# Splitting the sums of a slab's first pair of rows behind half of the down products, with five split weight pairs and four loaded tiles

## The chip, the cores and the metric

The kernel runs on one core of a Trainium2 chip. The metric is the device time of one execution in microseconds. The core has five engines with instruction queues of their own: TensorE (PE) for matmuls, with its weight loads shown as PEld, VectorE (DVE), ScalarE (ACT), GpSimd (POOL) and SyncE (SP), which here issues nearly all loads and stores. Each engine works through its queue in order, so an instruction that waits holds up all that stand behind it on its engine.

## The reference

One decoder layer for 1056 tokens (1024 of a prompt, eight sequences of four sampled tokens) of 1024 channels, in float32. Cut to what matters here:

```python
h = _rms(x, n_mix_pre); z = h @ w_in
m = concat([attention(q, k, v), pooling_mixer(u)]) @ w_out
x = x + _rms(m, n_mix_post)
f = _rms(x, n_ffn_pre)
f = (silu(f @ w_gate) * (f @ w_up)) @ w_down      # 1024 -> 2816 -> 1024
x = x + _rms(f, n_ffn_post)
x = x + sigmoid(x @ w_ple_gate) * (p @ w_ple)
```

It also returns the updated key, value and pooling windows.

## The kernel before, in words

**Numbers as pairs.** TensorE works on a rounded form of float32. To keep the precision, each operand is split into a rounded high part and the rest: `split(hi, lo, src)` (lines 163 to 165) is a copy on ACT (L164) and a subtraction on DVE (L165). A product then takes three matmuls: high by high, high by low, low by high. All of them come from line 126.

**Weights.** SP loads a weight tile of 512 KB into a `wr` tile; `W_RAW = 3` of these exist. A split turns it into a pair `wh`, `wl` of `wp` tiles; `2 * W_PAIRS = 8` of these exist. When a buffer is asked for again, the writer waits until the last reader of its former content is done. In the projections `weights(j, ahead=W_PAIRS - 1)` splits tiles ahead. In the channel sub-layer (FFN) the tiles are listed in `ITEMS`, and `need(k)` (lines 264 to 276) makes all items up to `LOOK = 4` beyond the one asked for.

**The FFN loop.** The tokens form three groups of 352; the first two share a scheme with seven instead of eight block products, the third is computed directly. The 22 blocks of 128 hidden channels form 11 slabs of two rows ("pairs" of a gate and an up weight; slot 0 and slot 1). `WALK` makes 16 visits: slabs 0 to 4 for the third group alone, slabs 5 to 10 for all three, then slabs 0 to 4 again for groups 0 and 1. Each row needs, for groups 0 and 1, sums of quarters of its gate and up weights: `w_sums` (lines 980 to 997) makes them by four POOL adds (L990) in place in the two loaded tiles, and splits both results (`sh` on ACT, `sl` on DVE). The adds can only start when the ordinary splits of the same tiles have read them.

A row is computed by `gate_up` (lines 1006 to 1069): products B11 and B21 of the gate weight, SiLU into `c`, for slot 0 then the *pending* down products of the visit before, then T4 with the up weight and S2, S3, S1, S4 with the sums. The adds of L1024 collect them from PSUM; the results are the hidden tiles `hid`, of group 0 (`hid<-c`) and of group 1 (`hid<-u`), split too. `downs(n)` (lines 1133 to 1143) runs over the output rows m = 0 to 3, then 4 to 7, and in each half over the groups 2, 0, 1; each product of six matmuls goes to one of eight PSUM banks, and DVE adds it to `o` (L1087), which frees the bank.

**Other work among it.** When the third group's last down products are done, the closing norm and the gate of that group (`ple_steps(2)`, with L1115 and L1119 on DVE) are issued a step at a time between the products; `turn` and `chain` count matmuls and DVE load for that. L1115 reads the broadcast norm factor from a PSUM bank.

**What sets the order.** The order of TensorE's matmuls is pinned to the written one. On the other engines, apart from a few pinned operations, a scheduler arranges the instructions when the program is built, from what they depend on and from its own estimates; their order can differ from the written one.

Of the kernel before, what the change touches and what calls it, by code (L numbers as in the profile page):

```python
# [47 lines left out]
UEXT = PST + DSEQ  # L48
ULEN = UPRE + SEQ + NDEC * UEXT

W_PAIRS = 4
W_RAW = 3


WARM = 8
# [6 lines left out]
def trunk_kernel(  # L62
# [31 lines left out]
    nc = tc.nc  # L94
# [11 lines left out]
    def nm(s):  # L106
        cnt[0] += 1
        return f"{s}{cnt[0]}"

    def act_tile(shape, dt=F32, s="a"):  # L110
        return apool.tile(shape, dt, tag="a", bufs=A_SLOTS, name=nm(s))
# [51 lines left out]
    def split(hi, lo, src):  # L163
        fix(se.copy(hi, src))  # L164
        fix(ve.tensor_tensor(lo, src, hi.bitcast(F32), op=ALU.subtract))  # L165
# [3 lines left out]
    def w_load(j):  # L169
        if j >= len(plan) or j in raws:  # L170
            return
        src, shape = plan[j]
        t = wpool.tile(shape, F32, tag="wr", bufs=W_RAW, name=nm("wr"))
        nc.sync.dma_start(t, src)
        raws[j] = t

    def w_tile(shape, s):
        return wpool.tile(shape, F32R, tag="wp", bufs=2 * W_PAIRS, name=nm(s))

    def w_split(j):  # L180
        if j >= len(plan) or j in pairs:
            return
        w_load(j)
        shape = plan[j][1]
        hi, lo = w_tile(shape, "wh"), w_tile(shape, "wl")
        split(hi, lo, raws[j])
        pairs[j] = (hi, lo)

    lazy = [False]

    def weights(j, ahead=W_PAIRS - 1):
        for i in range(j, j + (0 if lazy[0] else ahead) + 1):
            w_split(i)
            w_load(i + 1)
        return pairs[j]
# [19 lines left out]
    WALK += [(s, (0, 1)) for s in range(AHEAD)]  # L215
    ITEMS = []

    def item(kind, *js):
        ITEMS.append((kind, js))
        return len(ITEMS) - 1  # L220

    def direct_item(src, shape):
        return item("direct", add_plan(src, shape))

    WGU, WD = [], []
    for s, gs in WALK:
        pairs_of = []
        for i in range(SLAB):
            c = SLAB * s + i
            jg = direct_item(w_gu[c, 0], [P, KC, P])  # L230
            if 0 not in gs:
                ju = direct_item(w_gu[c, 1], [P, KC, P])
            if i == 0 and WD:
                last_s = WALK[len(WD) - 1][0]
                WD[-1] = [direct_item(w_dn[last_s, j], [P, SLAB, 512]) for j in range(2)]
            if 0 in gs:
                ju = direct_item(w_gu[c, 1], [P, KC, P])
            js = item("sums", jg, ju) if 0 in gs else None
            pairs_of.append((jg, ju, js))
        WGU.append(pairs_of)  # L240
        WD.append(None)
# [17 lines left out]
            wp = direct_item(w_ple[0], [P, 2, 512])  # L259
        WPE[1][m] = wp, direct_item(w_pg[m], [P, KC, P])  # L260

    made = {}

    def need(k, ahead=LOOK):

        for i in range(len(made), min(k + ahead + 1, len(ITEMS))):
            kind, js = ITEMS[i]
            if kind == "direct":
                w_split(js[0])
                made[i] = pairs[js[0]]  # L270
            else:
                made[i] = w_sums(*(raws[ITEMS[j][1][0]] for j in js))
            for kind, js in ITEMS[i + 1 : i + 3]:
                if kind == "direct":
                    w_load(js[0])
        return made[k]

    def gemm(ps, ops, start=True, stop=True):

        last = len(ops) - 1  # L280
        for i, (wh, wl, xh, xl) in enumerate(ops):
            mm(ps, wh, xh, start=start and i == 0, stop=False)
            mm(ps, wh, xl, start=False, stop=False)
            mm(ps, wl, xh, start=False, stop=stop and i == last)
# [56 lines left out]
    def load(dst, src):  # L341
        tc.keep_in_program_order(nc.sync.dma_start(dst, src))  # L342
# [38 lines left out]
    def u_load(c, h):  # L381
        j = U0[c]
        if h == 0:
            shape = plan[j][1]
            raws[j] = act_tile(shape) if c == 3 else wpool.tile(shape, F32, tag="wr", bufs=W_RAW, name=nm("wr"))
        load(raws[j][:, 4 * h : 4 * h + 4, :], plan[j][0][:, 4 * h : 4 * h + 4, :])
# [34 lines left out]
    for dst, src in ((psc, pscale), (skp, sink_p), (skd, sink_d)):  # L421
        load(dst, src)
    wpl = wpool.tile([P, 4, P], F32, tag="wr", bufs=W_RAW, name="wpl")
    nc.sync.dma_start(wpl, w_pool)
# [462 lines left out]
    def chain(steps, wait=0, alone=False):  # L887

        chains.append([steps, now[0] + wait, alone])
# [74 lines left out]
    for m in range(4, KC):  # L964
        out_proj(m, 1)
        need(0, m - 4)
        turn(24)
# [12 lines left out]
    def w_sums(a1, a2):  # L980


        a11, a12, a21, a22 = a1[:, 0:4, :], a1[:, 4:8, :], a2[:, 0:4, :], a2[:, 4:8, :]
        for out, a, b, op in (
            (a22, a21, a22, ALU.add),
            (a21, a11, a21, ALU.subtract),
            (a11, a22, a11, ALU.subtract),
            (a12, a12, a11, ALU.subtract),
        ):
            ge.tensor_tensor(out, a, b, op=op)  # L990
        two = []
        for src in (a1, a2):
            hl = w_tile([P, KC, P], "sh"), w_tile([P, KC, P], "sl")
            split(*hl, src)
            two.append(hl)
        (s24, s31) = two
        return {"S2": quarter(s24, 0), "S4": quarter(s24, 1), "S3": quarter(s31, 0), "S1": quarter(s31, 1)}

    def ops4(w, x):

# [2 lines left out]
    def quarter(w, h):  # L1003
        return tuple(t[:, 4 * h : 4 * h + 4, :] for t in w)

    def gate_up(items, slot, gs, pending):
# [16 lines left out]
        def add(out, a, ps):  # L1023
            ve.tensor_tensor(out, a, ps, op=ALU.add)  # L1024

        wg = need(ig)
        if 0 in gs:
            p1 = tmp(n, "p1")
# [8 lines left out]
        if pending and 0 in gs:  # L1037
            pending()
        wu = need(iu)
        if 2 in gs:  # L1040
            ve.tensor_tensor(sl, sl, direct(wu), op=ALU.mult)
# [59 lines left out]
    def ple_steps(g):  # L1101

        pl = half(g, F32R, "pl")
        pls[g] = pl[:, 0:2, :], pl[:, 2:4, :]
        raw = act_tile([P, 2, NS[g]])
        nc.sync.dma_start(raw, p[:, :, OFF[g] : OFF[g + 1]])
        x2s[g] = []
        for h in range(2):
            x2[g][h] = half(g, s="x2")
            nc.sync.dma_start(x2[g][h], x1d[g][h])  # L1110
        r = yield from rstd_steps(acc3[g])
        behind = tc.keep_in_program_order if g == 2 else lambda ins: ins
        for h in range(2):
            yh, xh = os_[g][h], x2[g][h]
            behind(ve.tensor_tensor(yh, yh, bc4(r), op=ALU.mult))  # L1115
            for c in range(4):
                k = 4 * h + c
                behind(
                    ve.scalar_tensor_tensor(  # L1119
                        xh[:, c, :], yh[:, c, :], gn[:, 3, k : k + 1], xh[:, c, :], op0=ALU.mult, op1=ALU.add  # L1120
                    )
                )
                if g == 2 and c % 2:
                    yield 6, 0
            yield 12 if g == 2 else 24, 0
            x2s[g].append(f_operand(xh, g))
            yield 10, 0
        split(*pls[g], raw)
        yield 6, 0
# [3 lines left out]
    def downs(n):  # L1133
        s, gs = WALK[n]
        hid[:] = old_hid
        for half_m in (range(4), range(4, KC)):
            for g in (2, 0, 1):
                for m in half_m:
                    if g in gs:
                        (last_down if g == 2 and s == NSLAB - 1 else down)(n, m, g)  # L1140
        if s == NSLAB - 1:
            share[0] = 0.1
            chain(ple_steps(2), 19)

    for n, (s, gs) in enumerate(WALK):
        if n == AHEAD:
            finish(list(chains))
        old_hid = list(new_hid)
        for i in range(SLAB):
            gate_up(WGU[n][i], i, gs, (lambda: downs(n - 1)) if i == 0 and n else None)  # L1150
# [126 lines left out]
```

## Time and profile before

| | before |
|---|---|
| median of 3 runs | 1118.11 us (1117.52 to 1119.99) |
| profiled execution | 1118.37 us |
| its span | 1116.6 us |
| mean granted TensorE clock | 0.998 |
| PE busy | 1106.5 us, 99% of the span |
| DVE busy | 748.3 us, 67% |
| ACT busy | 440.0 us, 39% |
| POOL busy | 179.4 us, 16% |
| read from and written to HBM | 88.30 MB and 10.11 MB |

The times in the profile count from the start of the span; 1.8 us of the execution lie around it. The channel sub-layer's first visits begin at about 220, the visits with groups 0 and 1 alone run from about 800 to 1000, and the last down products and the output part follow. In a row of the timeline stand the start, the duration, the engine, the line, the operation with its output and inputs, and in brackets the idle time of the engine before it with the instruction that ended it. In a row of waits stand who waited for whom, and then the sum, the number and the longest of these waits in us.

### The profile page before, as it was taken

Reading aid. Unit: us, or ns where it says so; the run is one execution under the profiler, and the core shown is the slowest. Engines: PE = TensorE matmul, PEld = TensorE weight load, DVE = VectorE, ACT = ScalarE, POOL = GpSimd, SP = SyncE. Lnnn points to the kernel's source line nnn. Section 1 sums busy time; section 2 is a strip of 40 time slices with the busy share of each in tenths; the row PEclk is TensorE's granted clock in tenths of the full one; section 3 lists DMA queues with packets and bytes.
Section 4 is the critical chain, followed back from the end, with each engine's and each line's share of the span. In section 5 each row is a group of like instructions: output and inputs, shape, how many; then the busy total and the mean of one; then the engine's idle time right before and its main releaser. Section 6 shows DMA issues by size and latency. Waiting matters only on the chain.

```text
span 1116.6 us, 17703 instructions
## 1 busy us (share of the span) xinstructions
PE 1106.5 (99%) x7171; PEld 1089.6 (98%) x7171; DVE 748.3 (67%) x1241; ACT 440.0 (39%) x779; POOL 179.4 (16%) x152
## 2 busy tenths in 40 slices
PE   8999999999999999999999999999999999999998
PEld 8999988899999999999999999999999999999998
DVE  6667478886979955255564555547887877789532
ACT  8323276664645523331222313123424334365220
POOL 0045032200000131011111102112132123100000
PEclk9999999999999999999999999999999999999999
DMA  8121311542543212121120202122112222336211
GB/s 289 56 71 38 122 43 38 194 157 85 203 166 129 99 38 76 39 76 39 38 60 17 78 36 76 38 100 79 57 58 83 70 76 80 124 133 222 85 58 39
DMA packets 35217, 99.54 MB, mean 89 GB/s; under 512 B 4132, under 2 KB 14660, under 8 KB 35136
## 3 DMA queue, kind: packets, MB, share of 16 engines
q1 hardware_dynamic: 33808, 96.65, 25.5%
q10 hardware_dynamic: 1328, 1.77, 0.5%
q8 instruction: 56, 0.92, 0.3%
q14 instruction: 25, 0.20, 0.1%
HBM read 88.30 MB, written 10.11 MB: 88 GB/s over the span
## 4 chain that ended last, share of the span: by engine, by line
PE 93%; DVE 3%; DMA 1%; issue 1%; POOL 1%; ACT 1%; SPq 0%; DVEq 0%; POOLq 0%
PE b L126 92%; PE b L120 1%; DMA xr<-in_x_dram 1%; DVE wl L165 1%; POOL wr L990 0%; SPq L342 0%; DVE h L368 0%; DVE o L1115 0%; DVE x L1119 0%; DVE mx L628 0%; DVE a L736 0%; DVE p L1024 0%; DVE hid L165 0%; ACT h L366 0%; ACT xr L377 0%
## 5 line engine op out<-in xcount | busy, mean ns | idle before, releaser
L126 PE MATMUL b<-fh,wh 128*128 128x352 f32 x808 | 260.7, 323 | 0.0
L126 PE MATMUL b<-fh,wl 128*128 128x352 f32 x808 | 259.3, 321 | 0.0
L126 PE MATMUL b<-fl,wh 128*128 128x352 f32 x808 | 259.0, 321 | 0.0
L126 PE MATMUL b<-hid,wh 128*128 128x352 f32 x1056 | 252.5, 322 | 1.8 <-DVE o L1115 1.2
L164 ACT CAST wh<-wr 128x1024 fp32r<-128x1024 f32 (+1 forms) x139 | 143.0, 1031 | 248.9 <-PE b L126 205.6
L165 DVE TENSOR_TENSOR wl<-wr,wh 128x1024 fp32r<-128x1024 f32 (+1 forms) x139 | 170.5, 1229 | 57.9 <-ACT wh L164 53.9
L126 PEld LDWEIGHTS b<-hid,wh 128*128 128x128 f32 x1056 | 182.3, 188 | 2.6 <-issue 1.5
L126 PE MATMUL b<-hid,wl 128*128 128x352 f32 x528 | 169.0, 320 | 0.0
L990 POOL TENSOR_TENSOR wr<-wr 128x512 f32<-128x512 f32 x44 | 63.4, 1441 | 623.0 <-DVE wl L165 621.3
L126 PEld LDWEIGHTS b<-fl,wh 128*128 128x128 f32 x808 | 151.9, 188 | 0.0
L126 PEld LDWEIGHTS b<-fh,wl 128*128 128x128 f32 x808 | 151.8, 188 | 0.0
L126 PEld LDWEIGHTS b<-fh,wh 128*128 128x128 f32 x808 | 151.6, 188 | 0.0
L1087 DVE TENSOR_TENSOR o<-o,b 128x352 f32<-128x352 f32 x240 | 114.9, 516 | 29.3 <-PE b L126 29.3
L126 PE MATMUL b<-fh,sh 128*128 128x352 f32 x352 | 113.6, 323 | 0.0
L126 PE MATMUL b<-fl,sh 128*128 128x352 f32 x352 | 112.7, 320 | 0.0
L126 PE MATMUL b<-fh,sl 128*128 128x352 f32 x352 | 112.7, 320 | 0.0
L126 PE MATMUL b<-h,wh 128*128 128x352 f32 x480 | 105.5, 325 | 0.9 <-ACT h L366 0.6
L165 DVE TENSOR_TENSOR sl<-wr,sh 128x1024 fp32r<-128x1024 f32 x44 | 53.8, 1222 | 75.5 <-ACT sh L164 75.5
L126 PEld LDWEIGHTS b<-hid,wl 128*128 128x128 f32 x528 | 98.9, 187 | 0.0
L164 ACT CAST sh<-wr 128x1024 fp32r<-128x1024 f32 x44 | 45.7, 1047 | 130.9 <-POOL wr L990 91.2
L126 PEld LDWEIGHTS b<-h,wh 128*128 128x128 f32 x480 | 81.9, 189 | 2.2 <-DVE h L368 1.2
L126 PE MATMUL b<-h,wl 128*128 128x352 f32 x240 | 66.3, 326 | 0.0
(150 smaller groups left out, 1591.0 us busy)
## 6 DMA issues: line engine op xcount, KB each, us to landing
wr<-in_w_gu_dram SPq DMA_DIRECT2D x64, 512.0 KB, 3.3
wr<-in_w_dn_dram SPq DMA_DIRECT2D x32, 512.0 KB, 3.3
wr<-in_w_pg_dram SPq DMA_DIRECT2D x14, 512.0 KB, 3.6
x<-in_x_dram SPq DMA_DIRECT2D x6, 704.0 KB, 7.1
x1d<-x SPq DMA_DIRECT2D x6, 704.0 KB, 3.5
x<-x1d SPq DMA_DIRECT2D x6, 704.0 KB, 6.7
out_y_dram<-yo SPq DMA_DIRECT2D x24, 176.0 KB, 1.9
wr<-in_w_out_b_dram SPq DMA_DIRECT2D x8, 512.0 KB, 3.3
```

What stands on the lines that cost most here:

```text
L120: ins = te.transpose(out, src, ident)
L126: ins = te.matmul(*args, **kw)
L164: fix(se.copy(hi, src))
L165: fix(ve.tensor_tensor(lo, src, hi.bitcast(F32), op=ALU.subtract))
L990: ge.tensor_tensor(out, a, b, op=op)
L1087: ve.tensor_tensor(o, o, v, op=ALU.add)
```

## The change

- `W_PAIRS` goes from 4 to 5: ten `wp` tiles instead of eight. `W_RAW` goes from 3 to 4. The default of `weights(ahead=...)` becomes 4.
- The splits of the sums move out of `w_sums` into `split_sums`. For the first row of each slab with sums (the set `BEHIND`) `need` only issues the adds and notes the item in `unsplit`; its splits are written after the first half of the down products (`split_unsplit()` at the end of each half), or when the sums are asked for.
- A buffer that the program sets aside for descriptors of software DMAs, of which the kernel uses none, goes from 16384 to 1024 bytes a partition; this makes the room for the three new tiles of 4096 bytes.

```diff
-W_PAIRS = 4
-W_RAW = 3
+W_PAIRS = 5
+W_RAW = 4
...
+    BEHIND = set()
...
             js = item("sums", jg, ju) if 0 in gs else None
+            if js and i == 0:
+                BEHIND.add(js)
...
-    made = {}
+    made, unsplit = {}, []
...
                 made[i] = w_sums(*(raws[ITEMS[j][1][0]] for j in js))
+                if i in BEHIND:
+                    unsplit.append(i)
+                else:
+                    split_sums(i)
             for kind, js in ITEMS[i + 1 : i + 3]:
                 if kind == "direct":
                     w_load(js[0])
+        if k in unsplit:
+            split_unsplit()
         return made[k]
+
+    def split_unsplit():
+        while unsplit:
+            split_sums(unsplit.pop())
...
             ge.tensor_tensor(out, a, b, op=op)
+        return a1, a2
+
+    def split_sums(i):
         two = []
-        for src in (a1, a2):
+        for src in made[i]:
             hl = w_tile([P, KC, P], "sh"), w_tile([P, KC, P], "sl")
             split(*hl, src)
             two.append(hl)
         (s24, s31) = two
-        return {"S2": quarter(s24, 0), "S4": quarter(s24, 1), "S3": quarter(s31, 0), "S1": quarter(s31, 1)}
+        made[i] = {"S2": quarter(s24, 0), "S4": quarter(s24, 1), "S3": quarter(s31, 0), "S1": quarter(s31, 1)}
...
                     if g in gs:
                         (last_down if g == 2 and s == NSLAB - 1 else down)(n, m, g)
+            split_unsplit()
...
-    nc = _bacc.Bacc("TRN2", target_bir_lowering=False, num_devices=1)
+    nc = _bacc.Bacc("TRN2", target_bir_lowering=False, num_devices=1, dynamic_dma_scratch_size=1024)
```

The line numbers of the changed kernel are some twenty higher than those before: the eviction of the down products, L1087 before, is L1104 there, L1115 is L1132, L1119 is L1136, and L1024 is L1041.

## The prediction

> **What bounds the kernel now.** I read the page's busy times first, then the chain that ended last in order of time, then TensorE's own waits, then windows by stage.
>
> ```profile
> PE 1106.5 (99%) x7171; PEld 1089.6 (98%) x7171; DVE 748.3 (67%) x1241; ACT 440.0 (39%) x779; POOL 179.4 (16%) x152
> ```
> ```profile
> 27.55 103.10 PE b L126 x646
> ...
> 219.61 587.17 PE b L126 x3722
> ...
> 817.51 28.43 PE b L126 x176
> ...
> 865.25 131.54 PE b L126 x830
> ...
> 1000.46 111.96 PE b L126 x701
> ```
> ```profile
> PE b L126 <- DVE o L1115: 1.2, 1, 1.2
> ...
> PE b L126 <- DVE hid L165: 0.6, 1, 0.6
> ```
> ```profile
> 400.00:600.00 200.00, 200.00 (x1261) 200.00 (x1260) 104.90 (x173) 56.92 (x90) 31.89 (x24) 1.00 0.16 51
> 600.00:800.00 200.00, 200.00 (x1263) 200.00 (x1263) 120.99 (x203) 59.05 (x88) 37.65 (x28) 1.00 0.18 60
> 800.00:820.00 20.00, 19.43 (x122) 18.96 (x120) 18.09 (x23) 7.90 (x12) 5.80 (x4) 1.00 0.23 79
> 820.00:870.00 50.00, 48.78 (x307) 48.52 (x307) 39.39 (x63) 16.84 (x22) 11.06 (x8) 1.00 0.22 74
> 870.00:1000.00 130.00, 129.64 (x820) 129.35 (x818) 102.16 (x170) 54.38 (x76) 27.61 (x20) 1.00 0.29 98
> 1000.00:1116.00 116.00, 112.37 (x702) 111.83 (x702) 63.82 (x97) 35.20 (x51) 0.00 (x0) 1.00 0.29 101
> ```
>
> TensorE (PE) is the bound: 99% busy, and the chain is five long stretches of matmuls. Window rows give busy time of PE, weight load, VectorE (DVE), ScalarE (ACT) and GpSimd (POOL). From 400 to 800 PE never pauses, while DVE is busy 52% and 60% of the time. Only in the five visits without the third group does DVE come near its limit: 102.16 of 130 us (79%), and 18.09 of 20 around 810. In the whole FFN loop PE waits twice, 0.6 us for a hidden tile and 1.2 us for the norm's product at L1115; the first needs these rows:
>
> ```profile
> 811.03 1.30 POOL L990 TENSOR_TENSOR wr<-wr 128x512 f32<-128x512 f32 x1 [16.49 <-DVE wl L165]
> ...
> 812.79 3.15 DVE L1119 SCALAR_TENSOR_TENSOR x<-o,c,x 128x352 f32<-128x352 f32 x2
> ...
> 815.85 1.60 DVE L165 TENSOR_TENSOR hid<-u,hid 128x352 fp32r<-128x352 f32 x1
> ...
> 817.51 0.43 PE L126 MATMUL b<-hid,wh 128*128 128x352 f32 x1 [0.57 <-DVE hid L165]
> ```
>
> The sums' adds run on POOL, and DVE's operations beside them are long: group 1's hidden takes 1.60 us, and comes 0.6 us too late for its down products. The second pause:
>
> ```profile
> 851.63 0.53 DVE L165 TENSOR_TENSOR hid<-c,hid 128x352 fp32r<-128x352 f32 x1
> ...
> 854.16 1.22 DVE L165 TENSOR_TENSOR wl<-wr,wh 128x1024 fp32r<-128x1024 f32 x1
> ...
> 855.51 1.45 POOL L990 TENSOR_TENSOR wr<-wr 128x512 f32<-128x512 f32 x1 [16.67 <-DVE wl L165]
> ...
> 859.95 1.28 POOL L990 TENSOR_TENSOR wr<-wr 128x512 f32<-128x512 f32 x1
> ...
> 861.27 1.05 ACT L164 CAST sh<-wr 128x1024 fp32r<-128x1024 f32 x1 [2.90 <-POOL wr L990]
> ...
> 862.35 1.23 DVE L165 TENSOR_TENSOR sl<-wr,sh 128x1024 fp32r<-128x1024 f32 x1 [3.71 <-ACT sh L164]
> ...
> 863.50 1.61 DVE L1115 TENSOR_TENSOR o<-o,b 128x1408 f32<-128x1408 f32 x1
> ...
> 865.25 0.56 PE L126 MATMUL b<-hid,wh 128*128 128x352 f32 x2 [1.22 <-DVE o L1115]
> ```
>
> The up weight's low half ends at 855.38, the four adds take 855.51 to 861.23, ACT's copy and DVE's subtraction follow, and L1115, queued behind the subtraction, frees its PSUM bank at 865.11. The subtraction stood 3.71 us at the head of DVE's queue. Deferring that split is the change's subject, so these two pauses are what it can win: 1.8 us, and some tenths of restart.
>
> **The change part by part.** *Instructions.* None is added or removed; PE's and POOL's orders are identical, those of ACT, DVE and SP (which issues the loads) differ. Work term: 0.
>
> *The deferral.* The split of the first pair's sums is written behind the first half of the downs. But the built DVE order is made by the scheduler. In the last slabs it was: hidden of group 1, the add of product B21 into c, two evictions o, sl, six o, sl, eight o. It becomes: hidden, c, sl, eight o, sl, eight o. The waiting subtraction thus stands *ahead* of the two evictions which it used to follow. So by itself the deferral wins nothing here; this added place is paid for below.
>
> *The fifth pair.* Every split can run one item earlier. In these slabs the up weight's split comes one step earlier, so the adds start earlier, and the next gate weight's split (formerly behind the downs) now stands ahead of group 1's hidden, inside the adds. A steady slab of this stage, before:
>
> ```profile
> 929.08 0.53 DVE L165 TENSOR_TENSOR hid<-u,hid 128x352 fp32r<-128x352 f32 x1 [0.55 <-ACT hid L164]
> ...
> 936.45 1.23 DVE L165 TENSOR_TENSOR wl<-wr,wh 128x1024 fp32r<-128x1024 f32 x1
> 937.59 0.51 DVE L1024 TENSOR_TENSOR p<-p,b 128x352 f32<-128x352 f32 x1
> 938.02 1.22 DVE L165 TENSOR_TENSOR wl<-wr,wh 128x1024 fp32r<-128x1024 f32 x1
> 939.15 0.52 DVE L1068 TENSOR_TENSOR u<-u,p 128x352 f32<-128x352 f32 x1
> 940.23 0.99 DVE L165 TENSOR_TENSOR hid<-u,hid 128x352 fp32r<-128x352 f32 x1 [0.55 <-ACT hid L164]
> ...
> 942.75 0.52 DVE L1087 TENSOR_TENSOR o<-o,b 128x352 f32<-128x352 f32 x1 [0.43 <-PE b L126]
> 946.22 1.23 DVE L165 TENSOR_TENSOR sl<-wr,sh 128x1024 fp32r<-128x1024 f32 x1 [2.95 <-ACT sh L164]
> 947.37 2.67 DVE L1087 TENSOR_TENSOR o<-o,b 128x352 f32<-128x352 f32 x6
> ```
> ```profile
> 944.46 0.48 PE L126 MATMUL b<-hid,wh 128*128 128x352 f32 x2
> ...
> 948.27 0.48 PE L126 MATMUL b<-hid,wh 128*128 128x352 f32 x2
> ```
>
> Walk: the up split takes the place at 936.45, the adds start about 937.75 instead of behind 939.24. The gate split follows at 938.1: alone 1.2 us; behind one add (1.45) 2.7. Then u (0.5 to 2.0), ACT's copy (0.55), hidden (0.5 to 1.6, the rows above): it ends between 940.9 and about 945, where PE opens group 1's products at 944.6 (the second matmul of the row at 944.46) and needs this half of the hidden three matmuls later, at 945.1. The adds take 5.7 us (855.51 to 861.23), so they end at 943.5, or 945.7 if DVE's three operations (1.22, 0.52, 0.53) hold them up in turn; copy and subtraction (1.1 and 1.2) end 945.8 to 948.0. The first eviction frees its bank 0.5 us later, at 946.3 to 948.5, and PE wants that bank for the ninth product, the eight banks being used in turn, at about 948.4 (the second matmul of the row at 948.27). Slack: between 2.1 us and nothing. I take no pause in the four steady slabs: 0, bounds 0 and 0.7 each (a late end of 0.1 plus a restart as large as L165's 0.57), so 0 to 2.8.
>
> [...]
>
> *The two pauses.* At 817 the gate split also goes ahead of the hidden, but the up split and so the adds end earlier. The hidden that ended at 817.45 ends at 816.7 at best and, with one split and one add more, at 820.1 at worst; nearest is the steady walk, where early adds and one more split cancel: 0, bounds -0.6 and +2.7. At 864 the built order puts the up split even ahead of group 0's hidden (851.63), so it is done at 852.9; the same walk then gives adds done at 858.7 to 860.9, subtraction at 861.0 to 863.2, two evictions (0.9) and L1115's 1.6: its bank is free at 863.5 to 865.7 instead of 865.11, and PE wants it at 863.7. I take the middle, 864.6: -0.5, bounds -1.4 and +0.6.
>
> *The fourth loaded tile.* One 512 KB weight load goes ahead of two loads of x at the start, where all transfers together bind:
>
> ```profile
> 26.19 1.54 ACT L366 ACTIVATE h<-xr,c 128x352 fp32r<-128x352 f32 x3
> 28.59 0.45 ACT L484 COPY acc<-b 128x352 f32<-128x352 f32 x1 [0.87 <-PE b L126]
> ```
> ```profile
> GB/s 289 56 71 38 122 43 38 194 157 85 203 166 129 99 38 76 39 76 39 38 60 17 78 36 76 38 100 79 57 58 83 70 76 80 124 133 222 85 58 39
> ```
>
> At 289 GB/s 512 KB are 1.8 us. The last x tiles feed ACT at 26.19, which then idles 0.87 before its next step. A delay beyond that hits PE: bounds 0 and 0.9; I take 0.1, as x had something in hand. In the attention part more weight loads go ahead of the caches, but each issues only when a tile comes free, at the same split as before; 0, bounds 0 and 1.2 (one split). In the slabs with three groups: 0, because DVE has 40% to spare from 600 to 800; if that cover were gone, each later split would cost its 1.2 us.
>
> Sum: 0 + 0 - 0.5 + 0.1 = -0.4 against the profiled 1118.37 us. That execution lies 0.26 over the median of the runs (1118.11), so about 1117.7; leaning to the rule above, I add 0.2 for each of four slabs: 1118.5. Its own range, from the bounds of the two pauses and the start, is 1116 to 1121.
>
> **Rivals.** *Both pauses go* (faster). The earlier adds let the subtraction and the hidden end before PE wants them: 1.2 + 0.6 less, and the tenths of restart, 1.9 to 2.2 in all: 1118.1 - 2.1 = 1116.0. It decides where the adds end before about 859.5. For it: that is inside my walk. Against: the gate split between the adds.
>
> *DVE binds the last slabs* (slower). With 79% busy and one long wait at the head of the queue, the eight evictions start too late, in four steady slabs and both transitions: six times 0.7 = 4.2 on the median: 1122.3. It decides where the subtraction ends after 948.0 in the walk above.
>
> *PE's pace.* From 600 to 800 there are 200/1263, 158.4 ns a matmul; the end runs 111.96/701, 159.7, and the first long stretch 103.10/646, 159.6, with a granted clock of 1.00 in every window above. A disturbance may leave the slow pace standing: 1.3 ns over 2500 matmuls is 3.2 us: 1121.3. Or it may mend the first and last stretch: 1347 times 1.3 ns, 1.7 us less. No row says what sets it.
>
> *The change does nothing:* the scheduler keeps the subtraction ahead of the evictions and PE has its tiles anyway: 1118.1.
>
> **How the numbers follow.** A measurement of this kernel can hardly tell 0.2% (2.2 us) from no change: the three runs span 2.5. My forecast 0.34; no effect 0.18; both pauses gone 0.17; DVE binds 0.21; slow pace 0.10. Of the pauses' rival half lies below 1115.9, with a mended pace or a little of the start; of my forecast a tenth; together 0.12, and 0.03 of the case of no effect for a mended pace: faster 0.15. Slower: nine tenths of DVE binding and of the slow pace, and a few hundredths of mine: 0.31. Same: 0.54. The range 1115.7 to 1122.6 leaves out 0.1 on each side.
>
> **What would show it.** In the changed trace: subtraction of the sums right behind c with a wait of 3 to 4.6 us (2.95 and 3.71 before); group 1's hidden of the last slabs ending 0 to 4 us later; no PE wait over 0.2 between 220 and 800; the wait for the norm's product at 0.3 to 1.5 us. I am wrong if PE has waits for evictions o in each late slab, if x loads hold up the first projection by over 1 us, or if PE's matmul interval changes over hundreds of microseconds.

## The result and the profile after

The changed kernel takes 1121.53 us (median of 8 runs, 1121.01 to 1122.69), the kernel before 1118.62 us beside it (8 runs, 1117.52 to 1120.59): the ratio is 1.0027, with a 95% interval of 1.0017 to 1.0036. It is slower by 2.9 us. The profiled execution took 1121.55 us, its span 1119.8 us, 3.2 us more than before.

Where the time went is best seen by comparing the starts of the same matmul, as both kernels issue 7171 of them in the same order. Up to the 5400th (about 827 us) the changed kernel is 0.9 us ahead. At the 5700th it is level (+0.05), at the 6000th 3.0 us behind, at the 6450th (995 us) 4.0, and at the end 3.2. All the loss lies in the last five visits; 0.8 of it comes back behind them. The waits of TensorE (who waited for whom: sum, number and longest in us):

```profile
PE b L126 <- DVE o L1104: 1.9, 2, 1.4
PE b L126 <- DVE hid L165: 1.7, 4, 0.6
...
PE b L126 <- ACT hid L164: 0.3, 1, 0.3
```

Before, the FFN loop had one wait for the norm's product (1.2) and one for a hidden tile (0.6). Now there are two waits for an eviction (1.4 near 863 and 0.5 near 909) and several for hidden tiles. The visit at 899 shows how they arise; its rows for TensorE, GpSimd and VectorE:

```profile
899.77 0.43 PE L126 MATMUL b<-hid,wh 128*128 128x352 f32 x1 [0.23 <-DVE hid L165]
...
904.05 0.42 PE L126 MATMUL b<-hid,wh 128*128 128x352 f32 x1 [0.34 <-ACT hid L164]
...
905.05 0.43 PE L126 MATMUL b<-hid,wh 128*128 128x352 f32 x1 [0.58 <-DVE hid L165]
...
908.96 0.59 PE L126 MATMUL b<-hid,wh 128*128 128x352 f32 x2 [0.46 <-DVE o L1104]
```
```profile
899.37 1.50 POOL L1004 TENSOR_TENSOR wr<-wr 128x512 f32<-128x512 f32 x1 [18.45 <-DVE wl L165]
900.94 3.67 POOL L1004 TENSOR_TENSOR wr<-wr,wr 128x512 f32<-128x512 f32 x2
904.69 1.44 POOL L1004 TENSOR_TENSOR wr<-wr 128x512 f32<-128x512 f32 x1
```
```profile
898.07 1.22 DVE L165 TENSOR_TENSOR wl<-wr,wh 128x1024 fp32r<-128x1024 f32 x1
899.20 0.52 DVE L165 TENSOR_TENSOR hid<-c,hid 128x352 fp32r<-128x352 f32 x1
...
900.07 1.87 DVE L165 TENSOR_TENSOR wl<-wr,wh 128x1024 fp32r<-128x1024 f32 x1
901.87 1.61 DVE L1085 TENSOR_TENSOR u<-u,p 128x352 f32<-128x352 f32 x1
904.03 0.97 DVE L165 TENSOR_TENSOR hid<-u,hid 128x352 fp32r<-128x352 f32 x1 [0.55 <-ACT hid L164]
...
907.25 1.23 DVE L165 TENSOR_TENSOR sl<-wr,sh 128x1024 fp32r<-128x1024 f32 x1 [1.82 <-ACT sh L164]
908.39 3.53 DVE L1104 TENSOR_TENSOR o<-o,b 128x352 f32<-128x352 f32 x8
```

The same visit before, with TensorE at the same place to 0.1 us; TensorE takes the new hidden of group 1 in the row at 902.99, its low half with the second matmul, at 903.15:

```profile
902.99 0.48 PE L126 MATMUL b<-hid,wh 128*128 128x352 f32 x2
```
```profile
899.05 1.45 POOL L990 TENSOR_TENSOR wr<-wr 128x512 f32<-128x512 f32 x1 [16.67 <-DVE wl L165]
```
```profile
895.18 0.53 DVE L165 TENSOR_TENSOR hid<-c,hid 128x352 fp32r<-128x352 f32 x1
...
897.70 1.22 DVE L165 TENSOR_TENSOR wl<-wr,wh 128x1024 fp32r<-128x1024 f32 x1
898.84 0.52 DVE L1068 TENSOR_TENSOR u<-u,p 128x352 f32<-128x352 f32 x1
899.91 0.98 DVE L165 TENSOR_TENSOR hid<-u,hid 128x352 fp32r<-128x352 f32 x1 [0.55 <-ACT hid L164]
...
901.25 0.94 DVE L1087 TENSOR_TENSOR o<-o,b 128x352 f32<-128x352 f32 x2
905.89 1.23 DVE L165 TENSOR_TENSOR sl<-wr,sh 128x1024 fp32r<-128x1024 f32 x1 [3.71 <-ACT sh L164]
```

In the changed kernel the up weight's split (898.07) stands ahead of group 0's hidden, which runs at 899.20 instead of 895.18 and is 0.2 us late. The adds start behind that split at 899.37, which is no earlier than before (899.05). The next gate weight's split, u and the hidden of group 1 then run beside the adds in 1.87, 1.61 and 0.97 us, and the hidden ends at 905.0 (900.9 before), when TensorE has waited for both of its halves. The adds, held up in turn, end at 906.1 (6.8 us after their start; 5.7 before). The subtraction follows and then all eight evictions, too late for the first bank.

The four waits sum to 1.6 us, but from the 5800th matmul to the 5900th the changed kernel falls from 0.05 to 2.78 us behind. The 1.1 us that the waits leave open go, by my estimate, with the restarts: at full pace a matmul starts 0.16 us after the one before it, while that one's row still runs (it is 0.32 us long), and a wait is counted only from the end of that row; and behind a wait the next matmul follows later, as in the row at 908.96, which takes 0.59 us where two matmuls at full pace take 0.48. The pace after them is slower, too. Windows of a stretch in which neither kernel waits, before and then after (length, and busy time with the number of instructions of PE, PEld, DVE, ACT and POOL):

```profile
912.00:996.00 84.00, 84.00 (x535) 84.00 (x534) 65.25 (x108) 35.40 (x51) 16.64 (x12) 1.00 0.33 112
```
```profile
912.00:996.00 84.00, 84.00 (x523) 84.00 (x522) 64.52 (x104) 32.51 (x48) 16.66 (x12) 1.00 0.34 118
```

In the changed kernel fewer matmuls begin in it, and the matmul-by-matmul comparison gives 1.0 us lost from the 6000th to the 6450th, at a granted clock of 1.00 in both. No run shows what sets this interval.

One thing got better: a group of 48 matmuls of the prompt's attention, before and after.

```profile
204.00 4.20 PE L126 MATMUL b<-a,a 128*64 128x256 f32 x48
```
```profile
203.88 3.66 PE L126 MATMUL b<-a,a 128*64 128x256 f32 x48
```

### The profile page after: what moved, and what is told of

It reads as the page before. It is cut to its first block, busy times and chain, and to the rows that moved or that the text cites. A ratio compares the mean times of both kernels' runs of the same rounds, so it can differ in the third digit from the quotient of the medians.

```text
span 1119.8 us, 17673 instructions
## 1 busy us (share of the span) xinstructions
PE 1108.0 (99%) x7171; PEld 1090.7 (97%) x7171; DVE 763.5 (68%) x1241; ACT 443.0 (40%) x779; POOL 190.7 (17%) x152
## 4 chain that ended last, share of the span: by engine, by line
PE 82%; issue 8%; POOL 3%; DMA 3%; DVE 3%; ACT 1%; SPq 0%; POOLq 0%; DVEq 0%
PE b L126 81%; POOL wr L1004 3%; DMA wr<-in_w_gu_dram 1%; PE b L120 1%; DMA xr<-in_x_dram 1%; DMA a<-in_dmask_dram 1%; DVE sl L165 1%; ACT sh L164 0%; SPq L356 0%; DVE h L382 0%; DVE mx L642 0%; DVE a L750 0%; ACT h L380 0%; ACT xr L391 0%; POOL a L656 0%
## 5 line engine op out<-in xcount | busy, mean ns | idle before, releaser
L165 DVE TENSOR_TENSOR wl<-wr,wh 128x1024 fp32r<-128x1024 f32 (+1 forms) x139 | 177.5, 1277 | 50.7 <-ACT wh L164 45.9
L1004 POOL TENSOR_TENSOR wr<-wr 128x512 f32<-128x512 f32 x44 | 60.4, 1374 | 616.6 <-DVE wl L165 614.9
L1104 DVE TENSOR_TENSOR o<-o,b 128x352 f32<-128x352 f32 x240 | 116.4, 516 | 37.2 <-PE b L126 36.9
L1004 POOL TENSOR_TENSOR wr<-wr,wr 128x512 f32<-128x512 f32 x44 | 70.4, 1600 | 3.4
```

The source lines that it names most:

```text
L1104: ve.tensor_tensor(o, o, v, op=ALU.add)
```

## The experiments

**Theory.** The order on DVE around the sums' adds sets the time: the fifth pair pulls splits into the adds and the waiting subtraction ahead of the evictions. **Rivals:** the deferral itself costs; the loaded tiles disturb the start; TensorE's pace changes by itself.

**Five pairs and four loaded tiles alone** (against the changed kernel):

```diff
-            if js and i == 0:
-                BEHIND.add(js)
```

> Five pairs and four loaded tiles alone, without the deferral. In the built DVE order of the last slabs both subtractions of the sums stand directly behind the hidden of group 1, ahead of all eight evictions; the next gate weight's split stands behind the first eight evictions. Theory (order of DVE around the adds): the hidden comes early again, so no wait for hidden near 900; but the evictions start behind two subtractions, so PE waits for a bank in each of three or four late slabs, 0.5 to 1.5 us each: 1120 to 1123 us. Rival (the deferral itself costs the time): 1118.6, as before. Rival (TensorE's pace alone): no wait of PE over 0.2 us, and the difference is made by matmul intervals of 161 ns in place of 159.

Measured: 1124.26 us against 1118.35, ratio 1.0057 [1.0044, 1.0069]. The time lies over the theory's 1120 to 1123. Without the deferral the loss is twice as large, so the deferral is not what costs; with five pairs it saves 2.7 us. The waits of this kernel, and windows around the longest of them:

```profile
PE b L126 <- DVE c L1039: 3.2, 1, 3.2
PE b L126 <- DVE o L1102: 2.1, 2, 1.7
```
```profile
863.00:870.00 7.00, 6.39 (x22) 6.39 (x23) 7.00 (x13) 1.54 (x2) 0.00 (x0) 0.51 0.44 150
870.00:895.00 25.00, 25.00 (x160) 25.00 (x159) 16.55 (x28) 7.99 (x11) 5.14 (x4) 1.00 0.13 43
```

Both subtractions stand ahead of c, and TensorE waits 3.2 us for it, up to 863.6: a wait that the theory had not named. From 863 to 870 the granted clock is 0.51. The waits for an eviction are two (1.7 near 912 and 0.4 near 955), not three or four. The wait for hidden near 900 is gone, as the theory has it; the one at 817 (0.9 here) is not.

**The deferral alone** (four pairs, three loaded tiles, the descriptor buffer at its former size):

```diff
-W_PAIRS = 5
-W_RAW = 4
+W_PAIRS = 4
+W_RAW = 3
```

> The deferral alone, with four pairs and three loaded tiles. In the built DVE order the first subtraction of the sums now stands behind eight evictions, and no gate split stands ahead of the hidden. Theory: the wait of 1.2 us for the norm's product near 865 goes, nothing comes in its place: 1116.6 to 1118, that is 0.6 to 2 us under before. Rival (the deferral itself costs): 1120 to 1121.5. Rival (pace): anywhere from 1117 to 1121 with no PE waits to explain it.

Measured: 1118.88 against 1118.35, ratio 1.0000 [0.9990, 1.0009], over the expected 1116.6 to 1118. VectorE's rows for the place of the second wait before:

```profile
858.41 0.51 DVE L1104 TENSOR_TENSOR o<-o,b 128x352 f32<-128x352 f32 x1
...
860.65 1.61 DVE L1132 TENSOR_TENSOR o<-o,b 128x1408 f32<-128x1408 f32 x1
...
865.77 1.21 DVE L165 TENSOR_TENSOR sl<-wr,sh 128x1024 fp32r<-128x1024 f32 x1
```

Here the deferral does what it says: the subtraction waits for nobody behind the evictions, the norm's product comes 2.9 us earlier than before (860.65 instead of 863.50), and TensorE no longer waits for it: 1.5 us gained there by the same matmul. The median does not show it. The runs lie between 1116.0 and 1120.6, and the profiled one, 1116.74, is among the fastest. So this kernel and the one before were each profiled a second time.

> The deferral alone once more, for a second profile, as its runs lie between 1116.0 and 1120.6 while the profiled one is 1116.7. If the spread is TensorE's pace, this profile shows the same PE waits but stretches of matmuls at another interval, worth the difference of the two spans; if it is the start or the attention part, the difference is made before 220 us.

> The kernel before once more, for a second profile: the waits at 817 and 865 should be there again with 0.6 and 1.2 us; what else differs from the first profile (start, attention, pace of the matmuls) is the spread of one and the same program, some 0.5 to 3 us.

Measured: 1117.79 and 1118.38 us, once each. The two profiles of the deferral alone have the same waits and nearly the same spacing of matmuls from 220 to 1000. They part before 33 us, by 1.6 us up to the 600th matmul; the first loses 0.6 again in the attention part, and 1.0 stays to the end. A window of 28 to 32 us in the first and in the second profile, and two of TensorE's waits in the second (the granted clock is the third number from the end):

```profile
28.00:32.00 4.00, 4.00 (x24) 3.81 (x25) 4.00 (x7) 3.38 (x9) 0.00 (x0) 1.00 0.00 0
```
```profile
28.00:32.00 4.00, 4.00 (x15) 4.00 (x15) 4.00 (x7) 3.48 (x8) 1.29 (x1) 0.50 0.00 0
```
```profile
23.55 0.79 PE L126 MATMUL b<-c,acc 128*88 128x1 f32 x8 [1.13 <-DVE acc L348]
...
27.39 1.00 PE L126 MATMUL b<-dg,c 88*128 88x352 f32 x2 [0.51 <-DVE dg L326]
```

So in these two the spread is the start. In the second execution the granted clock is 1.00 from 21 to 25 us, 0.61 from 25 to 28, 0.50 from 28 to 31 and 0.82 from 31 to 35; four matmuls in a row take 0.81 us at 21.62 and 1.31 at 25.57. So it falls 2 us after the wait of 1.13 us, which the first does not have, and before the wait of 0.51. In the first, the longest wait there, 1.01 us near 28, is followed by a granted clock of 1.00 from 28 to 35. The kernel before repeats its waits of 0.6 and 1.2 us to the tenth, and is 0.2 us later at the 300th matmul and 0.9 at the 1500th, level at the end. Whether the deferral alone gains its 1.5 us in the median stays open, as its interval is 2 us wide.

**The sums' splits pinned behind the first half's evictions** (changed kernel otherwise):

```diff
         while unsplit:
+            fixed[0] = True
             split_sums(unsplit.pop())
+            fixed[0] = False
```

> The changed kernel with the sums' splits pinned behind the first half's evictions on ACT and DVE; the next gate weight's split still stands ahead of group 1's hidden, inside the adds. Theory: the two waits for a bank (1.4 near 863 and 0.5 near 909) go; the waits for hidden (0.3 near 859, 0.2, 0.3 and 0.6 near 900 to 905) stay: 1118.5 to 1120. Rival (pace alone): waits may go, the time stays at 1121 or so.

```profile
PE b L126 <- DVE hid L165: 1.5, 3, 0.6
...
PE b L126 <- ACT hid L164: 0.3, 1, 0.3
```

Measured: 1118.26 against 1118.35, ratio 1.0003 [0.9994, 1.0012]: 3.3 us under the changed kernel. Both waits for an eviction are gone, those for hidden stay, as the theory has it; the time is slightly under its interval.

**The next gate weight's split behind group 1's hidden** in the last slabs:

```diff
-            if kind == "direct":
+            if kind == "direct" and i in GATES and anchor.get(1):
+                with tc.issue_after(anchor[1].ins):
+                    w_split(js[0])
+                made[i] = pairs[js[0]]
+            elif kind == "direct":
                 w_split(js[0])
```

Here `GATES` holds the gate items of slot 1 of the late visits, and `anchor[1]` is the last split of group 1's hidden.

> The changed kernel with the next gate weight's split queued behind group 1's hidden in the last slabs; the sums' subtraction still stands ahead of seven of eight evictions. Theory: without a fourth operation among the adds the hidden ends 2 to 3 us earlier and the adds about 1 us earlier: the waits for hidden near 859 and 900 to 905 go, the waits for a bank shrink to between 0 and 0.7 each: 1118 to 1119.5. Rival (the subtraction ahead of the evictions is all that matters): the bank waits stay at 1.4 and 0.5, 1120 to 1121.

```profile
PE b L126 <- DVE o L1111: 2.0, 2, 1.0
...
PE b L126 <- DVE o L1139: 0.4, 1, 0.4
PE b L126 <- DVE hid L166: 0.2, 1, 0.2
```

Measured: 1119.10 against 1118.35, ratio 1.0010 [1.0001, 1.0019], inside the expected interval. The waits for hidden fall to 0.2 as expected. Those for an eviction do not shrink to under 0.7: they are 1.0 each near 863 and 908, and the norm's product is waited for again. The theory had the adds end early enough; in fact the gate split only moves to a place behind the hidden that is still inside the adds, where it takes 2.31 us. So each order costs by itself: mending either alone leaves the other's waits.

**Both pins**, two times:

> The changed kernel with both pins: the sums' splits behind the first half's evictions, and the next gate weight's split behind group 1's hidden. Theory: all waits of PE near 859, 863 and 900 to 909 go, that near 817 (0.6) may shrink too; 1116.5 to 1118.3. Rival (the two orders are not all): waits of over 0.3 us stay between 850 and 950, 1119 to 1121.

> The changed kernel with both pins once more, for its interval against before: ratio 0.9982 to 0.9999, as measured, if the gain of the removed waits (2.2 us: 0.6, 1.2 and restarts) is real; 1.0 if the first sample was lucky in its start.

```profile
PE b L126 <- DVE dg L335: 1.4, 2, 1.0
...
PE b L126 <- DVE hid L166: 0.2, 1, 0.2
```

Measured: 1116.52 against 1117.78, ratio 0.9990 [0.9982, 0.9999], and 1117.13 against 1118.19, ratio 0.9988 [0.9979, 0.9997]. The waits of the late slabs, that at 817 among them, are gone but for 0.2 us near 896; those for dg lie at the start and at the output's norm. With the order mended, the five pairs and the deferral beat the kernel before by 1.1 to 1.3 us, and the changed kernel by about 4 to 5.

**The adds left out** in the last four visits (the sums are not formed there, part of the computation is missing; same DVE order as the changed kernel):

```diff
+            if not skip:
-            ge.tensor_tensor(out, a, b, op=op)
+                ge.tensor_tensor(out, a, b, op=op)
...
+                if n_walk > AHEAD + 6:
+                    LATE.add(js)
...
-w_sums(*(raws[ITEMS[j][1][0]] for j in js))
+w_sums(*(raws[ITEMS[j][1][0]] for j in js), skip=i in LATE)
```

> The changed kernel with the POOL adds of the first pair's sums left out in the last four visits (the weights' sums are then not formed there, so this part of the computation is missing); the order on DVE is that of the changed kernel. Theory (adds hold up DVE, and the subtraction that waits for them holds up the evictions): u, hidden and the gate split take 0.5, 0.5 and 1.2 us again, the subtraction waits under 1 us, all waits of PE between 810 and 950 go: 1116 to 1118. Rival (DVE has simply too much queued there): waits for hidden and evictions stay at over half their size, 1119.5 to 1121.

```profile
898.22 1.22 DVE L165 TENSOR_TENSOR wl<-wr,wh 128x1024 fp32r<-128x1024 f32 x1
899.36 0.52 DVE L1088 TENSOR_TENSOR u<-u,p 128x352 f32<-128x352 f32 x1
900.43 0.53 DVE L165 TENSOR_TENSOR hid<-u,hid 128x352 fp32r<-128x352 f32 x1 [0.55 <-ACT hid L164]
...
901.39 1.23 DVE L165 TENSOR_TENSOR sl<-wr,sh 128x1024 fp32r<-128x1024 f32 x1
902.53 3.63 DVE L1107 TENSOR_TENSOR o<-o,b 128x352 f32<-128x352 f32 x8
```

Measured: 1115.04 against 1117.78, ratio 0.9976 [0.9966, 0.9987], 1 us under the expected interval. The same operations in the same order take 1.22, 0.52 and 0.53 us instead of 1.87, 1.61 and 0.97, the subtraction waits for nothing, and no wait is left between 810 and 950. VectorE's amount of work there is not the cause. The adds are: they lengthen its operations, and the subtraction has to wait for their results.

**Five pairs with three loaded tiles, and four loaded tiles with four pairs** (both without deferral):

```diff
-            if js and i == 0:
-                BEHIND.add(js)
...
-W_RAW = 4          # the first kernel
+W_RAW = 3
...
-W_PAIRS = 5        # the second kernel
+W_PAIRS = 4
```

> Five pairs with three loaded tiles, no deferral: what the fifth pair does alone. The DVE order of the last slabs is that of five pairs and four loaded tiles without the deferral. Theory (the fifth pair sets that order, the fourth loaded tile is idle there): 1123 to 1125.5 us, with PE waits of 3 us near 863 and 1.5 to 2 near 912. Rival (the fourth loaded tile lets the splits run ahead): 1117.5 to 1119.

> Four loaded tiles with four pairs, no deferral. The DVE order of the last slabs is that of the kernel before. Theory: the waits of 0.6 near 817 and 1.2 near 865 as before, 1117.3 to 1119. Whether the 48 prompt attention matmuls near 204 take 3.7 us, as in the kernels with five pairs and four loaded tiles, or 4.2, as before, tells which of the two sizes made that difference. Rival (the fourth tile's loads disturb the start): 1 us more before 30 us, in every execution.

Measured: 1125.00, ratio 1.0055 [1.0040, 1.0071], and 1118.15, ratio 0.9996 [0.9987, 1.0005], both against 1118.19. The fifth pair makes the loss; the fourth loaded tile makes none, nor does the smaller descriptor buffer, which both of these kernels have. The 48 attention matmuls take 3.66 us in every kernel with five pairs, this one included, and 4.20 to 4.24 in every one with four, so the fifth pair also makes that gain of 0.5 us; by which wait was not tried. In the first of these kernels, a window behind a wait of 2.2 us for an eviction:

```profile
912.00:925.00 13.00, 11.28 (x61) 11.28 (x62) 11.29 (x21) 2.95 (x4) 0.00 (x0) 0.87 0.25 82
```

**Both pins, and the up weight's split behind group 0's hidden** in the late slabs:

```diff
-        s = need(is_)
+        s = need(is_, LOOK - 1 if slot and 2 not in gs else LOOK)
...
-                with tc.issue_after(anchor[1].ins):
+                with tc.issue_after(anchor[0 if i in UPS else 1].ins):
...
+            if i == 0 and n_walk > AHEAD + 6:
+                GATES.add(ju)
+                UPS.add(ju)
```

> Both pins, and the up weight's split of the late slabs queued behind group 0's hidden. Theory: the last wait of the late slabs (0.2 near 896) and its restart go, 0.6 us under both pins alone: 1115.3 to 1117. Rival: with the up split later, the adds end later and the subtraction's wait comes back at the evictions: waits for o, 1117 to 1118.5.

Measured: 1117.48, ratio 0.9992 [0.9983, 1.0001]. The wait near 896 goes, and waits of 0.2 us for an eviction and for c come in its place: the rival's way, and no gain over both pins alone. Part of this is pace: in its profile the slower interval is there again and costs 1.2 us from the 5900th matmul to the 6450th, behind waits of only 0.2 us, while with both pins alone that stretch costs nothing. No run separates the two.

## Why the prediction was right or wrong

The range of 1115.7 to 1122.6 held the time, and the likeliest case did not come: 1118.5, no change that can be measured, against 1121.53. Slower had 0.31. The rival "DVE binds the last slabs" named the late evictions and comes near the time with 1122.3, but that is partly luck: it had six waits for evictions, and there were two; the rest is waits for hidden tiles and pace, and the load of VectorE is not the cause. The forecast's "own range" of 1116 to 1121 does not follow from the bounds either: those of the two pauses and the start reach 1122.3, and 1125.1 with the slabs.

- *What can be gained: the two pauses.* Right. Where both pins end them, the same matmul comes 0.8 us earlier at 817 and 1.4 at 865, 2.2 in all, as forecast for both pauses. Of that 1.1 stays at the 6000th matmul: 0.4 goes between the pauses, without a wait, and 0.6 around the wait near 896. The medians give 1.3 and 1.1 us.
- *The deferral cancelled by the built order.* Right in the order (c, then the subtraction, then eight evictions), and the wait at its head is shorter than predicted (1.82 and 1.83 us, not 3 to 4.6), since the operations ahead of it took the time. "So by itself the deferral wins nothing here" was wrong: against five pairs without it, it saves 2.7 us, because there both subtractions stand ahead; and with four pairs it ends the wait at 865.
- *"I take no pause in the four steady slabs".* This is the step that failed. I walked the slab at 940 and took it for the others, of which there is one and not three: behind the two transitions only the visits at 899 and 940 have the adds of a first pair in them. At 940 the walk held: the hidden ends at 947.4, inside its bounds when these are moved with TensorE (3.3 us later there), and there is no wait. But that slab was the roomier one. Before the change TensorE wants the low half of the hidden 5.7 us after the adds' start at 940 (939.37, 945.1) and 4.1 us after it at 899 (899.05, 903.15). In the changed kernel the gate split, u and the hidden, all three beside the adds, end 5.4 and 5.6 us after that start. And "so the adds start earlier", which was to pay for the gate split, did not come true at 899 (899.37 after 899.05). This slab cost 2.7 us, against a bound of 0.7: the bound had one late end of 0.1 and one restart, and there were four waits of 0.2 to 0.6 with 1.1 us of restarts.
- *The pause at 864: -0.5 taken, bounds -1.4 and +0.6.* Measured +0.9 by the same matmul, 0.6 of it at a wait for a hidden tile at 859, which the sum did not have, and 0.4 at the bank. I timed the bank of the norm's product, wanted at 863.7. In the new order the two evictions wait too, and their bank is wanted at 861.8: TensorE waited 1.4 us for it. That bank was missing from the sum. The pause at 817 did stay (0.63 after 0.57).
- *GpSimd and VectorE: 0.2 us more for each of four slabs.* No run shows this term. In the slab at 899 the gate split and u took 1.87 and 1.61 us beside the adds, and 1.22 and 0.52 with the adds left out; that slab cost 2.7 us, and at 940 TensorE did not wait. c, with an input from PSUM, takes 0.51 us beside an add (904.92 in the changed kernel).
- *The start: 0.1, bounds 0 and 0.9.* Not to be told: two executions of one program differ by 1.6 us there, with a granted clock of 1.00 in the one and 0.50 in the other from 28 to 32 us.
- *The attention part: 0.* Wrong by -0.5 us, the 48 matmuls.
- *The signs named.* No wait lies between 220 and 800, as said. Waits for evictions came, but at two places and not in each late slab; the wait for the norm's product, expected at 0.3 to 1.5 us, is gone, as TensorE had already waited for the evictions' bank.
- *PE's pace, as a rival by itself.* In part: 1.0 us from 912 to 996, behind the waits, of which 0.8 comes back by the end. In the long stretch from 220 to 800 the matmuls have the same starts to 0.1 us in both kernels.

## What to carry to other kernels

More buffers let a scheduler start work earlier, and on an engine that works in order early work stands ahead of urgent work: read the built order, and the room that TensorE leaves, in every stage and not in one, before taking a bigger pool as free. Where GpSimd works beside VectorE, read from the trace how long each VectorE operation takes there (here the gate split took 1.87 us instead of 1.22 and u 1.61 instead of 0.52, beside four adds of 6.8 us in all, and an addition with an input from PSUM 0.51). A split whose source is late is best pinned behind the work that frees PSUM banks; here two pins turned a loss of 2.9 us into a gain of 1.1 to 1.3.

## What the runs showed of the hardware

The granted clock fell at some of TensorE's pauses and not at others. With five pairs and four loaded tiles alone, it was 1.00 from 855 to 863 us and 0.51 from 863 to 870, where a wait of 3.2 us ends at 863.6. With five pairs and three loaded tiles, a wait of 2.2 us ends at 913.7: the clock was 0.87 from 912 to 925, and the matmuls from 914.33 to 917.26 were 0.29 us apart instead of 0.16. In the same execution a wait of 2.9 us ends at 867.2, and the clock stayed at 1.00 from 863 to 870. At the start of the second execution of the deferral alone, a wait of 1.1 us ended at 23.55, with eight matmuls of one column behind it, and the clock was 0.61 from 25 to 28 and 0.50 from 28 to 31. No run moved a pause alone, so what decides is not shown.

The waits of the changed kernel near 900 cost more than their length: four waits of 1.6 us in all made 2.7, and 1.2 more came from the pace behind them up to the 6450th matmul.
